# Two-layer hybrid encoder: the first product pair starts from the raw input, and the row factor goes into its eviction

## The chip, the core and the metric

One core of one Trainium2 chip runs the whole program. Its engines are named as in the profile: PE (TensorE, with PEld for its weight loads and PEq for its sequencer), DVE (VectorE), ACT (ScalarE), POOL (GpSimd) and SP (SyncE, which here only issues DMAs). The metric is the device time of one execution in microseconds (us), smaller is better. Before the change the median of three runs is 1521.92 us (1521.45 to 1524.45).

## The reference, cut to what matters

Two layers of one mixer. Each layer normalises the 512 x 2048 input by rows, multiplies it with one wide input projection, and runs three mixers on the parts. The change touches the beginning of layer 0 alone: the norm and the first part of the projection.

```python
def rmsnorm(x, g):
    x32 = x.astype(jnp.float32)
    y = x32 * lax.rsqrt(jnp.mean(x32 * x32, axis=-1, keepdims=True) + EPS)
    return (y * g.astype(jnp.float32)).astype(x.dtype)

h = rmsnorm(x, pre_norm_g[l])
z = h @ w_in[l]
q_lat, kv_lat, k_pe, gb, gc, xin, q_mem, gate = split_cols(z)
c_out = short_gated_conv(gb, gc, xin, conv_w[l])
```

The row factor (one number for each token, `r`) stands in front of a row of `h`. So a product of `h` with any block of `w_in` is the product of the unscaled rows with that block, each row of the result multiplied by its factor.

## The kernel before

**Numbers in two parts.** Every fp32 operand is split into a rounded part (`hi`, fp32r) and the rest (`lo`): ACT casts (L177 for weights, L257 for inputs), DVE subtracts (L178, L258). A product is three matmuls (`mm3`, L252 to L254): input hi x weight hi, input hi x weight lo, input lo x weight hi. The input tile is what PE loads (PEld), the 512 weight columns stream.

**Products.** The tokens are four tiles of 128; `x0` to `x3` in the code, t = 0 to 3. The projection is computed in groups of two column blocks with a seven-product scheme: the 2 x 2 blocks A11, A12, A21, A22 of the normalised transposed input (A11 = token tiles 0 and 1, first 1024 features; A12 = the same tokens, last 1024 features; A22 = token tiles 2 and 3, last 1024 features) and the sums S1 to S4 of them. Product P1 reads A11, P2 A12, P5 S1, P6 S2, P3 S4, P7 S3, P4 A22. Each product of a group is four steps (`c` = 0 to 3), each with one unit of weights of 256 rows by 512 columns (`wr` raw, `wh` and `wl` its parts) and 12 matmuls: 6 for the first token tile of the pair (`tt` = 0) and 6 for the second. For the first two groups, "first pair", the program runs P1 and P2 of group 0, then P1 and P2 of group 1, then P5 of group 0 and the rest. With `by_two` the first two steps of a product go together, so that 12 matmuls for tile 0 come before those for tile 1. Product P1 of such a group is copied out of PSUM by ACT (L464); the others are added by DVE.

**The beginning of layer 0.** PE runs 60 transposes of the identity (`warm`, L1208) while the input is on its way. For each token tile: SP loads all of `x` (L604), ACT sums the squares (L563), POOL makes `r` (L262, L264), DVE multiplies the rows by it (`hs`, L613, in halves of 1024), PE transposes quarters of four 128 x 128 blocks (`hps`, L582), and the eviction multiplies by the norm's gain (`hT`, by DVE L584 for token tiles 0 and 1, by ACT L588 for the second tile's first half and for tiles 2 and 3). Then A11 and A12 are split (L257, L258). The gains come from rows that ACT's queue loads (L281 to L283) and that one transpose turns (L291, L293).

**Order.** Each engine takes its own instructions strictly in the order of the program. PE, SP and POOL follow the order in which the steps are written (`add`, `put`); so do DVE and ACT until `first.close`, which stands behind the first step of P1. After that a scheduler orders DVE and ACT. Weight units are loaded 8 raw buffers deep, split two units ahead into 3 hi and 3 lo buffers; the sums S1 to S4 of token tiles 2 and 3 are put into a queue (`defer`) and given out between steps.

Of the kernel before, what the change touches and what calls it, by code (L numbers as in the profile page):

```python
# [5 lines left out]
F32 = mybir.dt.float32  # L6
# [6 lines left out]
P = 128  # L13
# [194 lines left out]
def encoder(tc, x, mem, positions, pre_norm_g, w_in, q_norm_g, w_uq, kv_norm_g, w_ukv, conv_w,  # L208
# [62 lines left out]
    def setup():  # L271
        ident = scrap("ident", P)
        make_identity(nc, ident)
        identr = const.tile([P, P], F32R, name="identr")
        nc.vector.tensor_copy(identr, ident)
# [3 lines left out]
        rows = scrap("rows", P)[:KT * 2 * depth + 12 * depth]  # L279
        n = KT * depth  # L280
        nc.scalar.dma_start(rows[:n], pre_norm_g.rearrange("l (k p) -> (l k) p", p=P))  # L281
        nc.scalar.dma_start(rows[n:2 * n], mem_norm_g.rearrange("l (k p) -> (l k) p", p=P))
        nc.scalar.dma_start(rows[2 * n:], conv_w.rearrange("l k (c p) -> (l k c) p", p=P))  # L283
        G["rows"] = rows

    def turn_constants():
        rows = G["rows"]
        n = KT * depth
        m = 2 * n + 12 * depth
        ps = bank("cps")  # L290
        nc.tensor.transpose(ps[:, :m], rows, G["ident"][:m, :m])  # L291
        cols = const.tile([P, m], F32, name="cols")
        nc.vector.tensor_copy(cols, ps[:, :m])  # L293
        for l in range(depth):
            G[f"g1_{l}"] = cols[:, l * KT:(l + 1) * KT]
            G[f"gm_{l}"] = cols[:, n + l * KT:n + (l + 1) * KT]
            G[f"cw{l}"] = cols[:, 2 * n + 12 * l:2 * n + 12 * (l + 1)].rearrange("p (k c) -> p k c", k=3)
# [72 lines left out]
    class Left:  # L370
# [8 lines left out]
        def split(self, name, p, src):  # L379
            t = self.ops[name, p] = slab(f"{name}{p}", F32R)  # L380
            c = src.shape[-1]
            split_to(t[:, :1024].rearrange("p (k c) -> p k c", c=c), t[:, 1024:].rearrange("p (k c) -> p k c", c=c), src)
# [33 lines left out]
    def group(left, key, w, block, slot, passes, final, hold=None, by_two=False):  # L416
# [185 lines left out]
    def first_load(t):  # L602
        xt = G[f"x{t}"] = slab("x")
        nc.sync.dma_start(xt, x[0, t * P:(t + 1) * P, :])  # L604
# [5 lines left out]
    def first_rows(t, halves=(0, 1)):  # L610
        for h in halves:
            c = slice(h * 1024, (h + 1) * 1024)
            nc.vector.tensor_scalar_mul(G[f"hs{t}"][:, c], G[f"x{t}"][:, c], G[f"r{t}"])  # L613


    def projection(l):
# [33 lines left out]
        def own_lat():  # L650
# [5 lines left out]
        L = G["left"]  # L656
        gs = [
            group(L, (l, 0), 512, block((O_GC, O_XI), 512), slot_of("gc", "xi"), HEAD, fin_u, by_two=l == 0),
# [445 lines left out]
    def out_proj(l):  # L1104
# [62 lines left out]
        g1 = group(G["left"], ("o", l, 1), 512, block(1), slot(1), LATE, fin(1), hold if last else None)  # L1167
# [72 lines left out]
    G["src"], G["dst"] = x[0], None  # L1240
    for l in range(depth):
# [7 lines left out]
        if l == 0:  # L1249
            add(use)  # L1250
            def turn_half(t, h, on=None):
                return lambda: transpose_rows(0, t, G[f"hs{t}"], (2 * h, 2 * h + 1), on)
# [29 lines left out]
        if l == 0:  # L1282
            put(a[:1])
            add(first.close)
            add(turn_half(1, 1))
            add(lambda: left_half(0, (1,)))
            add(lambda: left_half(1, (1,)))
            add(lambda: first_rows(2))
# [112 lines left out]
```

## Time and profile before

| | us |
|---|---|
| median of three runs | 1521.92 |
| the profiled execution's own time | 1524.04 |
| its span in the trace | 1522.3 |
| PE busy | 1491.2 |
| DVE busy | 1092.2 |
| ACT busy | 862.6 |

The span runs from the first to the last recorded instruction; 1.74 us of the profiled execution lie outside it. Times in the views are from the start of the span. A row of the timeline gives start, duration, engine, source line, operation, output and inputs, and in brackets how long the engine stood idle before and which instruction it waited for. Rows that overlap by a little are normal: an engine starts the next instruction before the last has drained, so that the distance between two starts, not the duration, is what a queue of them costs.

### The profile page before, as it was taken

The numbers are of one execution on the slowest core, as the hardware profiler recorded it, in microseconds if no ns is written. First come the engines' busy times: TensorE is split into PE (matmuls) and PEld (weight loads), VectorE is DVE, ScalarE is ACT, GpSimd is POOL, SyncE is SP. The second block draws the span as 40 slices with busy tenths as digits, with TensorE's granted clock in tenths as the row PEclk, the third lists the DMA queues.
The fourth block names the chain that finished last, engine by engine and source line by source line (L and its number), as shares of the span: only waits on it lengthen the run. The fifth ranks groups of instructions, "written<-read, shape, count | busy, mean of one in ns | idle before, by whom it ended". The sixth has DMA issues, their size and how long they took to land.

```text
span 1522.3 us, 20192 instructions
## 1 busy us (share of the span) xinstructions
PE 1491.2 (98%) x7613; PEld 1278.4 (84%) x7613; DVE 1092.2 (72%) x1446; ACT 862.6 (57%) x1335; POOL 258.6 (17%) x265
## 2 busy tenths in 40 slices
PE   9999999999999999999999999999999999998997
PEld 7788888988898888878788888888988888887885
DVE  6965675565968668979788766675566586698787
ACT  7733534454767768645688434434454686774543
POOL 1233131332000000010310333131332000000011
PEclk9999999999999999999999999999999999999999
DMA  8999898989581112165977999897999411022845
GB/s 332 217 221 223 197 173 172 204 192 261 155 273 59 42 42 71 35 164 156 322 277 247 236 229 226 183 177 167 195 211 221 130 59 40 29 84 62 240 100 180
DMA packets 138229, 258.80 MB, mean 170 GB/s; under 512 B 16828, under 2 KB 39700, under 8 KB 134804
## 3 DMA queue, kind: packets, MB, share of 16 engines
q0 software_dynamic: 52544, 116.41, 39.3%
q1 hardware_dynamic: 85456, 141.07, 28.7%
q8 instruction: 59, 0.97, 0.2%
q14 instruction: 38, 0.31, 0.1%
q10 hardware_dynamic: 132, 0.05, 0.0%
HBM read 242.81 MB, written 14.68 MB: 169 GB/s over the span
## 4 chain that ended last, share of the span: by engine, by line
PE 85%; DVE 7%; ACT 4%; issue 2%; DMA 2%; POOL 1%; DVEq 0%; POOLq 0%; ACTq 0%
PE P L253 20%; PE P L254 20%; PE P L252 20%; PE ptp L1002 2%; DVE wl L178 2%; PE tps L758 2%; DMA wr<-in_w_o_dram 1%; PE o L253 1%; PE sc L252 1%; PE sc L253 1%; PE sc L254 1%; PE o L254 1%; PE o L252 1%; PE sc L982 1%; PE sc L983 1%
## 5 line engine op out<-in xcount | busy, mean ns | idle before, releaser
L178 DVE TENSOR_TENSOR wl<-wr,wh 128x1024 fp32r<-128x1024 f32 (+1 forms) x400 | 475.8, 1195 | 286.5 <-ACT wh L177 284.6
L177 ACT CAST wh<-wr 128x1024 fp32r<-128x1024 f32 (+1 forms) x400 | 411.0, 1032 | 476.6 <-PE P L254 391.3
L253 PE MATMUL P<-wl,S 128*128 128x512 f32 (+1 forms) x896 | 345.2, 385 | 7.1 <-DVE wl L178 7.1
L252 PE MATMUL P<-wh,S 128*128 128x512 f32 (+1 forms) x896 | 347.0, 387 | 1.2 <-ACT wh L177 1.2
L254 PE MATMUL P<-wh,S 128*128 128x512 f32 (+1 forms) x896 | 344.0, 384 | 0.0
L137 POOL DMA_DIRECT2D wr<-in_w_in_dram x160 | 193.4, 1209 | 484.0 <-DVE wl L178 405.9
L252 PE MATMUL P<-wh,A 128*128 128x512 f32 (+1 forms) x656 | 253.1, 386 | 0.6 <-ACT wh L177 0.6
L253 PE MATMUL P<-wl,A 128*128 128x512 f32 (+1 forms) x656 | 251.9, 384 | 1.5 <-DVE wl L178 1.5
L254 PE MATMUL P<-wh,A 128*128 128x512 f32 (+1 forms) x656 | 251.7, 384 | 0.5 <-DVE A L258 0.5
L253 PEld LDWEIGHTS P<-wl,S 128*128 128x128 f32 x896 | 168.7, 188 | 39.0 <-DVE wl L178 9.7
L252 PEld LDWEIGHTS P<-wh,S 128*128 128x128 f32 x896 | 168.5, 188 | 31.7 <-ACT wh L177 2.2
L254 PEld LDWEIGHTS P<-wh,S 128*128 128x128 f32 x896 | 168.6, 188 | 30.5
L253 PEld LDWEIGHTS P<-wl,A 128*128 128x128 f32 x656 | 123.2, 188 | 23.7 <-DVE wl L178 2.1
L254 PEld LDWEIGHTS P<-wh,A 128*128 128x128 f32 x656 | 123.2, 188 | 23.3 <-DVE A L258 1.2
L252 PEld LDWEIGHTS P<-wh,A 128*128 128x128 f32 x656 | 123.1, 188 | 23.0 <-ACT wh L177 1.4
L988 ACT ACTIVATE P<-sc,nm 128x512 f32<-128x512 f32 (+1 forms) x96 | 59.9, 624 | 33.3 <-DVE nm L985 32.8
L1118 POOL DMA_DIRECT2D g<-in_post_norm_g_dram x8 | 5.5, 809 | 368.6 <-PE ptp L1002 368.6
L991 ACT ACTIVATE P<-P,rec 128x512 f32<-128x512 f32 (+1 forms) x96 | 62.1, 658 | 5.1 <-DVE rec L990 5.1
L985 DVE TENSOR_REDUCE nm<-sc 128x1 f32<-128x512 f32 (+1 forms) x96 | 57.3, 597 | 9.9 <-PE sc L983 6.3
L258 DVE TENSOR_TENSOR PT<-ptp,PT 128x512 fp32r<-128x512 f32 (+1 forms) x96 | 56.6, 595 | 4.9 <-ACT PT L257 4.5
L182 ACT ACTIVATE wh<-wr,cols 128x512 fp32r<-128x512 f32 x64 | 44.2, 721 | 20.0 <-PE mk L253 7.5
L183 DVE SCALAR_TENSOR_TENSOR wl<-wr,cols,wh 128x512 fp32r<-128x512 f32 x64 | 46.4, 750 | 12.3 <-ACT wh L182 10.9
(273 smaller groups left out, 2268.1 us busy)
## 6 DMA issues: line engine op xcount, KB each, us to landing
wr<-in_w_in_dram POOLq DMA_DIRECT2D x128, 512.0 KB, 6.9
wr<-in_w_in_dram SPq DMA_DIRECT2D x112, 512.0 KB, 5.6
wr<-in_w_o_dram SPq DMA_DIRECT2D x56, 512.0 KB, 4.6
wr<-in_w_in_dram POOLq DMA_DIRECT2D x32, 416.0 KB, 5.7
wr<-in_w_in_dram SPq DMA_DIRECT2D x24, 416.0 KB, 4.3
wr<-in_w_mk_dram SPq DMA_DIRECT2D x16, 512.0 KB, 5.1
wr<-in_w_mv_dram SPq DMA_DIRECT2D x16, 512.0 KB, 5.2
wr<-in_w_o_dram POOLq DMA_DIRECT2D x16, 512.0 KB, 7.0
```

Source lines behind the costliest of these rows:

```text
L137: engine.dma_start(dst, src, **kw)
L177: nc.scalar.copy(hi[:, :n], src)
L178: nc.vector.tensor_tensor(lo[:, :n], src, hi[:, :n].bitcast(F32), op=ALU.subtract)
L182: nc.scalar.activation(hi[:, h], src[:, h], AF.Copy, scale=g)
L183: nc.vector.scalar_tensor_tensor(lo[:, h], src[:, h], g, hi[:, h].bitcast(F32), op0=ALU.mult, op1=ALU.subtract)
L252: nc.tensor.matmul(ps, ah, bh, start=first, stop=False, **kw)
L253: nc.tensor.matmul(ps, ah, bl, start=False, stop=False, **kw)
L254: nc.tensor.matmul(ps, al, bh, start=False, stop=last, **kw)
L258: nc.vector.tensor_tensor(lo, src, hi.bitcast(F32), op=ALU.subtract)
L985: nc.vector.tensor_reduce(nmax, ps, axis=AX.X, op=ALU.max, negate=True)
L988: nc.scalar.activation(pt, ps, AF.Exp, bias=nmax, accum_out=tot)
L991: nc.scalar.activation(pt, pt, AF.Copy, scale=rec)
```

## The change

The names of the lines shift by up to 62 between the two programs; tile names stay.

- **Loads.** `x0` and `x1` are loaded in halves of 1024 features, and the weight units come between them: x0 first half, unit 0, x1 first half, unit 1, x0 second half, unit 2, x1 second half, unit 3, and so on. The gains of the memory norm and the convolution's weights move from ACT's queue to SP's, behind `x3`, and are turned later (`other_constants`, after P2 of group 0).
- **P1 of group 0** takes A11 from the raw, unscaled `x`, transposed and multiplied by the gain alone, and split by quarters. ACT's eviction of this product multiplies by `r` in place of a copy.
- **Factors.** The sums of squares of `x0` and `x1`, and the scaling of their second halves for A12, come after that.
- **A11 anew.** `spread_factors` builds, from diagonal matrices and a matrix of ones, a 128 x 256 tile of factors in PSUM by four matmuls (`rps`); `scale_half` multiplies the raw A11 (`hT`) by it on DVE, and A11 is split a second time for all products that follow.
- **PE.** 20 and 8 `warm` transposes in place of 60; the transposes of A12 come after the third step and after the last step of P1; `by_two` now also holds for P2 of group 0.

```diff
+        if len(halves) == 2:
+            nc.sync.dma_start(G[f"x{t}"], x[0, t * P:(t + 1) * P, :])
+        for h in halves if len(halves) == 1 else ():
+            c = slice(h * 1024, (h + 1) * 1024)
+            nc.sync.dma_start(G[f"x{t}"][:, c], x[0, t * P:(t + 1) * P, c])
...
-                if apart:
+                if apart and factor:
+                    nc.scalar.activation(s[1, 0], ps, AF.Copy, scale=factor(tt))
+                elif apart:
                     nc.scalar.copy(s[1, 0], ps)
...
-            if by_two and k == 0:
+            if by_two and k < 2:
...
+    def spread_factors():
+        ps = G["rows01"] = bank("rps")
+        for t in range(2):
+            work = scrap("diag", dt=F32R)
+            ones, dh, dl = (work[:, k * P:(k + 1) * P] for k in range(3))
+            d = scrap("factors", P)
+            nc.vector.tensor_scalar(ones, G["ident"], 0.0, 1.0, op0=ALU.mult, op1=ALU.add)
+            nc.vector.tensor_scalar_mul(d, G["ident"], G[f"r{t}"])
+            nc.vector.tensor_copy(dh, d)
+            nc.vector.tensor_tensor(dl, d, dh.bitcast(F32), op=ALU.subtract)
+            for k, part in enumerate((dh, dl)):
+                nc.tensor.matmul(ps[:, t * P:(t + 1) * P], ones, part, start=k == 0, stop=k == 1)
+
+    def scale_half(t):
+        h = G[f"hT{t}"][:, :8, :]
+        r = G["rows01"][:, t * P:(t + 1) * P].rearrange("p (o c) -> p o c", o=1).broadcast_to([P, 8, P])
+        nc.vector.tensor_tensor(h, h, r, op=ALU.mult)
...
+    add(lambda: first_load(0, (0,)))
+    add(pr.begin_loads(1))
+    add(lambda: first_load(1, (0,)))
+    add(pr.begin_loads(2))
     for t in range(2):
-        add(lambda t=t: first_load(t))
-        add(lambda t=t: first_factor(t))
-        if t == 0:
-            add(lambda: first_rows(0))
-    add(pr.begin_loads(3))
+        add(lambda t=t: first_load(t, (1,)))
+        add(pr.begin_loads(3 + t))
+    add(pr.begin_loads(6))
     add(lambda: first_load(2))
-    add(pr.begin_loads(5))
+    add(pr.begin_loads(8))
     add(lambda: first_load(3))
-    add(lambda: warm(60))
-    add(turn_constants)
+    add(constants_load)
+    add(lambda: warm(20))
+    add(pre_gains)
...
-            add(turn_half(0, 0))
-            add(lambda: first_rows(1, (0,)))
-            add(pr.begin_prep(1))
-            add(lambda: left_half(0, (0,)))
-            add(pr.begin_prep(2))
-            add(turn_half(1, 0, nc.scalar))
-            add(lambda: first_rows(1, (1,)))
-            add(lambda: left_half(1, (0,)))
-            add(pr.begin_prep(3))
-            add(lambda: first_factor(2))
-            add(turn_half(0, 1))
+            add(turn_raw(0, 0))
+            add(turn_raw(0, 1))
+            add(split_raw(0, 0))
+            add(pr.begin_prep(1))
+            add(split_raw(0, 1))
+            add(lambda: warm(8))
+            add(turn_raw(1, 0))
+            add(pr.begin_prep(2))
+            add(turn_raw(1, 1, nc.scalar))
+            add(split_raw(1, 0))
+            add(split_raw(1, 1))
+            add(pr.begin_prep(3))
+            add(lambda: first_factor(0))
...
             put(a[:1])
             add(first.close)
-            add(turn_half(1, 1))
-            add(lambda: left_half(0, (1,)))
-            add(lambda: left_half(1, (1,)))
-            add(lambda: first_rows(2))
-            add(lambda: first_factor(3))
-            add(lambda: first_rows(3))
-            put(a[1:], b[:1])
+            add(lambda: first_rows(0, (1,)))
+            add(lambda: first_factor(1))
+            add(lambda: first_rows(1, (1,)))
+            put(a[1:2])
+            add(turn_half(0))
+            add(lambda: left_half(0, (1,)))
+            put(a[2:])
+            add(turn_half(1))
+            add(lambda: left_half(1, (1,)))
+            add(spread_factors)
...
+            put(b[:1])
+            for t in range(2):
+                add(lambda t=t: scale_half(t))
+                add(lambda t=t: left_half(t, (0,)))
             add(turn[2])
             add(lambda: right_half(0))
-            put(b[1:3])
+            put(b[1:2])
             add(turn[3])
             add(lambda: right_half(1))
-            put(b[3:])
+            put(b[2:])
+            add(other_constants)
```

Three places show how DVE's queue moves. Names carry numbers that differ between the programs: `hT` is a transposed token tile, `A` a part of A11 or A12 (or A22), `S` a part of S1 to S4, `P` a product's PSUM bank.

DVE at its beginning; `hs` are scaled rows, `A` the low part of A11. Before:

```order
L613 TENSOR_SCALAR hs_102<-x_100,r_107 128x1024 x2
L293 COPY cols<-cps_195 128x88
L584 TENSOR_TENSOR hT_199<-hps_200,cols 128x512
L584 TENSOR_TENSOR hT_199<-hps_206,cols 128x512
L613 TENSOR_SCALAR hs_113<-x_111,r_118 128x1024
L178 TENSOR_TENSOR wl_214<-wr_120,wh_213 128x1024
L258 TENSOR_TENSOR A_20_217<-hT_199,A_20_217 128x1024
```

Now:

```order
L293 COPY colsrows<-cps_148 128x32
L598 TENSOR_TENSOR hT_152<-hps_153,colsrows 128x512
L598 TENSOR_TENSOR hT_152<-hps_159,colsrows 128x512
L258 TENSOR_TENSOR A_13_165<-hT_152,A_13_165 128x512
L641 TENSOR_SCALAR diag_334<-identr 128x128
L178 TENSOR_TENSOR wl_169<-wr_100,wh_168 128x1024
L258 TENSOR_TENSOR A_13_165<-hT_152,A_13_165 128x512
```

The two row scalings that waited for `r` are gone from the front; the first scaling now stands behind the third weight unit's low part.

DVE between the A12 splits and token tile 2's first work (`A_57` in the changed program, `A_50` before, is the part of A22 that is made from token tile 2). Before:

```order
L258 TENSOR_TENSOR A_38_324<-hT_224,A_38_324 128x1024
L613 TENSOR_SCALAR hs_329<-x_132,r_334 128x1024 x2
L178 TENSOR_TENSOR wl_363<-wr_272,wh_362 128x1024
L178 TENSOR_TENSOR wl_383<-wr_274,wh_382 128x1024
L178 TENSOR_TENSOR wl_444<-wr_276,wh_443 128x1024
L178 TENSOR_TENSOR wl_465<-wr_278,wh_464 128x1024
L258 TENSOR_TENSOR A_50_437<-hT_400,A_50_437 128x1024
```

Now:

```order
L258 TENSOR_TENSOR A_36_330<-hT_183,A_36_330 128x1024
L652 TENSOR_TENSOR hT_152<-hT_152,rps_333 128x1024
L632 TENSOR_SCALAR hs_350<-x_116,r_355 128x1024 x2
L652 TENSOR_TENSOR hT_183<-hT_183,rps_333 128x1024
L632 TENSOR_SCALAR hs_359<-x_122,r_364 128x1024 x2
L258 TENSOR_TENSOR A_13_165<-hT_152,A_13_165 128x1024
L258 TENSOR_TENSOR A_18_203<-hT_183,A_18_203 128x1024
L178 TENSOR_TENSOR wl_452<-wr_120,wh_451 128x1024
L178 TENSOR_TENSOR wl_456<-wr_221,wh_455 128x1024
L258 TENSOR_TENSOR A_57_445<-hT_408,A_57_445 128x1024
```

Two multiplications by the factors in PSUM and two more subtractions for A11 stand in front of the weights of P1 of group 1.

DVE in front of product P5 of group 0, whose second token tile reads `S_67` before and `S_77` now (S1 made from token tile 3). Before:

```order
L178 TENSOR_TENSOR wl_655<-wr_518,wh_654 128x1024
L397 TENSOR_TENSOR hT_481<-hT_481 128x1024
L397 TENSOR_TENSOR hT_481<-hT_224,hT_481 128x1024
L178 TENSOR_TENSOR wl_672<-wr_540,wh_671 128x1024
L258 TENSOR_TENSOR S_67_688<-hT_481,S_67_688 128x1024
```

Now:

```order
L178 TENSOR_TENSOR wl_650<-wr_511,wh_649 128x1024
L408 TENSOR_TENSOR hT_474<-hT_474 128x1024
L178 TENSOR_TENSOR wl_669<-wr_537,wh_668 128x1024
L408 TENSOR_TENSOR hT_474<-hT_183,hT_474 128x1024
L178 TENSOR_TENSOR wl_689<-wr_558,wh_688 128x1024
L469 TENSOR_TENSOR gb_535<-gb_535,P_71_629 128x512
L469 TENSOR_TENSOR gb_535<-gb_535,P_72_630 128x512
L178 TENSOR_TENSOR wl_708<-wr_580,wh_707 128x1024
L258 TENSOR_TENSOR S_77_720<-hT_474,S_77_720 128x1024
```

Two more weight units and two additions of P2's result now stand ahead of that S1 subtraction. Some 80 rows into DVE's queue, and at the matching places of the other engines, the two programs come to the same order and keep it to the end.

More of the change, by code (lines that the diff above doesn't have):

```diff
@@ L377, in __init__, with split @@
             self.ops = {}
-        def split(self, name, p, src):
-            t = self.ops[name, p] = slab(f"{name}{p}", F32R)
+        def split(self, name, p, src, ks=slice(None)):
+            if (name, p) not in self.ops:
+                self.ops[name, p] = slab(f"{name}{p}", F32R)
             c = src.shape[-1]
-            split_to(t[:, :1024].rearrange("p (k c) -> p k c", c=c), t[:, 1024:].rearrange("p (k c) -> p k c", c=c), src)
+            hi, lo = (self.ops[name, p][:, h * 1024:(h + 1) * 1024].rearrange("p (k c) -> p k c", c=c) for h in range(2))
+            split_to(hi[:, ks], lo[:, ks], src)
         def there(self, name, kt, tt):
@@ L414, in encoder, with group @@
     LATE = [["P2"], ["P1"], ["P5", "P6", "P3"], ["P7"], ["P4"]]
-    def group(left, key, w, block, slot, passes, final, hold=None, by_two=False):
+    def group(left, key, w, block, slot, passes, final, by_two=False, factor=None, hold=None):
         bk = {}
@@ L600, in right_half, with first_load @@
         combine(left, tt, a[:, :8, :], a[:, 8:, :], b[:, :8, :], b[:, 8:, :])
-    def first_load(t):
-        xt = G[f"x{t}"] = slab("x")
-        nc.sync.dma_start(xt, x[0, t * P:(t + 1) * P, :])
+    def first_load(t, halves=(0, 1)):
+        if f"x{t}" not in G:
+            G[f"x{t}"] = slab("x")
+        if len(halves) == 2:
[3 more added lines that the diff above has]
+            nc.sync.dma_start(G[f"x{t}"][:, c], x[0, t * P:(t + 1) * P, c])
     def first_factor(t):
@@ L656, in projection @@
         L = G["left"]
+        rf = (lambda tt: G[f"r{tt}"]) if l == 0 else None
         gs = [
-            group(L, (l, 0), 512, block((O_GC, O_XI), 512), slot_of("gc", "xi"), HEAD, fin_u, by_two=l == 0),
+            group(L, (l, 0), 512, block((O_GC, O_XI), 512), slot_of("gc", "xi"), HEAD, fin_u, l == 0, rf),
             group(L, (l, 1), 512, block((O_GB, O_G + 1024), 512), slot_of("gb", "gg"), HEAD, fin_g),
@@ L1166, in out_proj @@
         g0 = group(G["left"], ("o", l, 0), 512, block(0), slot(0), MERGED, fin(0))
-        g1 = group(G["left"], ("o", l, 1), 512, block(1), slot(1), LATE, fin(1), hold if last else None)
+        g1 = group(G["left"], ("o", l, 1), 512, block(1), slot(1), LATE, fin(1), hold=hold if last else None)
         return g0, g1, gains, fetch
```

42 lines of the change are left out of this document (26 added, 16 removed).

## The prediction

> **What bounds the kernel now.** I read the page's busy times first, then busy time in stretches of 10 us, then the timelines of PE, DVE and ACT up to 80 us, because from DVE's eightieth row on the two programs order their work alike. The page:
>
> ```profile
> span 1522.3 us, 20192 instructions
> PE 1491.2 (98%) x7613; PEld 1278.4 (84%) x7613; DVE 1092.2 (72%) x1446; ACT 862.6 (57%) x1335; POOL 258.6 (17%) x265
> ```
>
> Over the whole span PE is the bound: 31 us of its time are idle. The stage that is changed reads differently. Columns: the stretch, the sum, then busy PE, PEld, DVE, ACT, POOL (with counts), the granted PE clock, the DMA share, GB/s.
>
> ```profile
> 10.00:20.00 10.00, 7.92 (x50) 6.29 (x49) 8.73 (x12) 8.87 (x16) 0.74 (x2) 1.00 1.03 402
> ...
> 40.00:50.00 10.00, 9.05 (x39) 6.94 (x38) 9.65 (x10) 8.30 (x21) 2.62 (x2) 1.00 0.82 180
> 50.00:60.00 10.00, 10.00 (x46) 8.26 (x45) 9.65 (x10) 7.63 (x9) 2.43 (x2) 1.00 1.02 271
> 60.00:70.00 10.00, 10.00 (x46) 8.29 (x45) 9.93 (x10) 5.83 (x6) 3.62 (x3) 1.00 1.07 244
> 70.00:80.00 10.00, 10.00 (x46) 8.29 (x45) 9.55 (x10) 6.19 (x7) 3.68 (x4) 1.00 1.12 196
> 80.00:90.00 10.00, 10.00 (x46) 8.29 (x45) 4.90 (x4) 3.38 (x4) 4.80 (x4) 1.00 1.11 195
> ```
>
> From 40 to 80 us DVE is as full as PE; its first slack is 5.1 us at 80 to 90. So the beginning has two limits, PE's start and the sum of DVE's rows. The rows that fix them, first PE's:
>
> ```profile
> 1.61 4.70 PE L1208 MATMUL warm<-identr 128*128 128x128 f32 x21 [1.61 <-DVE identr L275]
> 1.61 8.96 PE L1208 MATMUL warm<-identr 128*128 128x128 f32 x60 [1.61 <-DVE identr L275]
> 13.13 1.96 PE L582 MATMUL hps<-identr,hs 128*128 128x128 f32 x16 [1.61 <-DVE hs L613]
> 14.85 0.47 PE L252 MATMUL P<-wh,A 128*128 128x512 f32 x1
> 27.66 0.39 PE L252 MATMUL P<-wh,A 128*128 128x512 f32 x1
> 49.12 0.50 PE L253 MATMUL P<-wl,A 128*128 128x512 f32 x1 [0.76 <-DVE wl L178]
> 65.14 0.39 PE L254 MATMUL P<-wh,A 128*128 128x512 f32 x1
> 65.36 0.39 PE L252 MATMUL P<-wh,S 128*128 128x512 f32 x1
> 76.24 0.39 PE L252 MATMUL P<-wh,S 128*128 128x512 f32 x1
> ```
>
> P1 starts at 14.85, P2 at 27.66, P5 of group 0 at 65.36 and P6 at 76.24; between matmuls lie 0.2267 us. Now DVE, from its first scaling to the subtraction for which P5's second token tile waits:
>
> ```profile
> 8.68 1.42 DVE L613 TENSOR_SCALAR hs<-x,r 128x1024 f32<-128x1024 f32 x2 [7.12 <-POOL r L264]
> 11.12 1.29 DVE L584 TENSOR_TENSOR hT<-hps,cols 128x512 f32<-128x512 f32 x2 [0.19 <-PE hps L582]
> 12.33 0.75 DVE L613 TENSOR_SCALAR hs<-x,r 128x1024 f32<-128x1024 f32 x1
> 12.99 1.22 DVE L178 TENSOR_TENSOR wl<-wr,wh 128x1024 fp32r<-128x1024 f32 x1
> 14.12 1.22 DVE L258 TENSOR_TENSOR A<-hT,A 128x1024 fp32r<-128x1024 f32 x1
> 37.03 1.23 DVE L178 TENSOR_TENSOR wl<-wr,wh 128x1024 fp32r<-128x1024 f32 x1 [2.95 <-ACT wh L177]
> 63.27 1.22 DVE L258 TENSOR_TENSOR S<-hT,S 128x1024 fp32r<-128x1024 f32 x1
> 64.40 1.22 DVE L178 TENSOR_TENSOR wl<-wr,wh 128x1024 fp32r<-128x1024 f32 x1
> 65.54 1.28 DVE L457 TENSOR_TENSOR gb<-gb,P 128x512 f32<-128x512 f32 x2
> ```
>
> The distance of starts is what a queue costs: 1.13 us for a subtraction of 1024 columns (12.99 to 14.12), 0.66 for a row scaling (12.33 to 12.99), 0.605 for an eviction of 512 (two in 11.12 to 12.33), 0.6 for a product's addition. That S1 subtraction ends at 64.5. P5's eighth matmul after its start is the first that reads it, at 65.36 + 8 x 0.2267 = 67.2. Before, DVE is 2.7 us ahead there.
>
> **The change part by part: PE's start.** Both loads and squares stand on ACT's timeline:
>
> ```profile
> 5.72 1.91 ACT L563 ACTIVATE hs<-x 128x2048 f32<-128x2048 f32 x1 [2.13 <-DMA x<-in_x_dram]
> 8.41 1.92 ACT L563 ACTIVATE hs<-x 128x2048 f32<-128x2048 f32 x1 [0.68 <-DMA x<-in_x_dram]
> 12.45 1.05 ACT L257 CAST A<-hT 128x1024 fp32r<-128x1024 f32 x1 [1.10 <-DVE hT L584]
> 13.40 1.06 ACT L177 CAST wh<-wr 128x1024 fp32r<-128x1024 f32 x1
> 31.83 4.24 ACT L588 ACTIVATE hT<-hps,cols 128x128 f32<-128x128 f32 x16
> 35.83 1.17 ACT L177 CAST wh<-wr 128x1024 fp32r<-128x1024 f32 x1
> ```
>
> `x0` is there at 5.72 and `x1` 2.69 us later, so half of `x0` should be there 1.35 us earlier, at 4.4. The 20 `warm` transposes last until about 6.0 (21 take 4.70 us); four transposes (0.5), an eviction (0.69 with 0.2 of wait) and the cast of a quarter (0.5, half of the 0.95 between 12.45 and 13.40) bring it to 8.0, unit 0's cast to 9.0: there the first matmul starts, in place of 14.85. That is 5.85 us for PE. Without them 1.4 us of PE work is added (8 `warm` at 0.11 by the rows above, 39 taking 4.26 us, and four small `rps` matmuls): if PE never waited for more than before, the kernel would gain about 4.9 us.
>
> It will wait, and I walked each in-order queue with those distances. The low part of unit 0 is ready at 10.3, of unit 1 at 12.6; the third step runs 16.5 to 19.2. The squares of `x0` stand on ACT behind three weight casts, so `r` of `x0` comes only at 16.4: the square starts at 13.4, and from a square's start to the scaling lie 2.96 us (5.72 to 8.68). The fourth step waits for its low part until 22.85. The `rps` matmuls of the second token tile wait for DVE's last diagonal row, which stands behind the evictions and the split of A12, until 26.5; P2, behind them on PE, starts at 26.75 and not at 27.66. So the 5.85 us have shrunk to 0.9. In P1 of group 1 the second token tile needs the PSUM bank that P2's additions free, at 44.2; its last low part is ready at 51.85. P5 starts at 65.3, level with before.
>
> **DVE's sum.** Before, 55.7 us pass from 8.68 to 64.40. In them stand 17 weight subtractions, 11 of inputs and 6 combinations (L397), 34 x 1.135 = 38.6; 8 scalings, 5.4; 6 evictions, 3.6; 2 additions, 1.2; `cols`, 0.25. Some of these groups, up to 66 us, with the count, busy us and mean ns, and the idle time before them with its cause (the eighteenth weight subtraction is the one at 64.40):
>
> ```profile
> L178 DVE TENSOR_TENSOR wl<-wr,wh 128x1024 fp32r<-128x1024 f32 x18 | 21.7, 1220 | 3.5 <-ACT wh L177 3.5
> L613 DVE TENSOR_SCALAR hs<-x,r 128x1024 f32<-128x1024 f32 x8 | 5.7, 750 | 8.0 <-POOL r L264 8.0
> L275 DVE CAST identr<-ident 128x128 fp32r<-128x128 f32 x1 | 0.2, 228 | 1.3 <-POOL ident masks.py:199 1.3
> L293 DVE COPY cols<-cps 128x88 f32<-128x88 f32 x1 | 0.2, 250 | 0.6 <-PE cps L291 0.6
> ```
>
> Together 49.0; 6.7 us are waits and gaps. Now, to the same subtraction:
>
> - added: two multiplications by the factors. No row of before multiplies 1024 columns by a PSUM operand. Nearest are the eviction (0.605 for 512, so 1.21) from above and 1.135 from below; I take 1.2 each: +2.4.
> - two more A11 subtractions, done first by quarters: 4 quarters at 0.57 (half of 1.135) instead of none, while the two whole ones stay: +2.3.
> - eight rows of 128 x 128 for the diagonals: such a cast lasts 0.23 (`identr`), and starts lie up to 0.1 closer than durations (0.66 against 0.75 for a scaling), so 0.13 to 0.23; I take 0.175: +1.4, 1.0 to 1.8.
> - one eviction more (+0.6), a second `cols` (+0.2), two row scalings less (-1.3).
> - two weight subtractions and two additions now stand ahead of this row that stood behind it: 2 x 1.135 + 2 x 0.6 = +3.5.
>
> That is 58.0, 9.0 more, of which 5.5 is new work and 3.5 moved. DVE begins, with `cols`, at 6.3, when `warm` and its transpose are over, and not at 8.68: -2.4. Its waits I put at 4.8 instead of 6.7: 0.6 before the first weight, 1.6 for `r` of `x0`, 0.4 for `r` of `x1` and 0.4 for that of `x2`, 1.5 for a weight whose cast stands on ACT behind the 16 evictions that take 4.0 us at 31.83, 0.3 for the rest. So the subtraction ends at 6.3 + 58.0 + 4.8 + 0.1 = 69.2 against the 65.3 + 1.8 = 67.1 at which P5 needs it: PE stands for 2.1 us, in a place where it did not stand before.
>
> What the change does to SP's queue costs nothing:
>
> ```profile
> 5.72 0.34 SPq L604 DMA_DIRECT2D x<-in_x_dram x1
> ```
>
> four issues more take 1.4 us while the transfers, 2.69 us for 1 MB, are the slower part and hide them (uncovered, 1.4 us), and the gains that leave ACT's queue are needed only after P2. What waits behind P5's matmul on PE is everything to the end of layer 0, so the delay stays. The two weights and two additions are already done then, so DVE itself is only 4.7 - 3.5 = 1.2 late afterwards, less than PE, and the 5.1 us of slack at 80 to 90 take that up. The price of the change is 2.1 - 0.06 = +2.0 us.
>
> **By the Trainium skill.** The PE clock opened during `warm`: 0.224 us each for the first 21, 0.109 for the other 39. The Trainium skill, "TensorE: Matmul & The Clock Gate", Part 4, says that the clock gate does not engage for transposes, which do not count as busy; by that 20 transposes would open nothing and the first matmuls would run at half pace. The trace disagrees: it opened with transposes alone.
>
> **Rivals.**
>
> R1, DVE hardly waits. If the squares and casts of ACT come early enough, the early start is kept: with no wait at all the subtraction ends at 64.4, PE meets P5 unhindered, and what remains is DVE's bound, 4.8 us below the forecast: -2.8; with half of my waits, -0.4. 1519.1 to 1521.5. For it: ACT loses the two squares from its front. Against: `r` feeds two scalings and a diagonal now, and ACT is 8.3 of 10 busy at 40 to 50.
>
> R2, slower: the PE clock closes in the sparse stretch between 9 and 27, where PE has to stand six times, up to 2.5 us at `rps`. Half pace costs 0.11 us a transpose in `warm`'s first part, and if 20 matmuls of 0.2267 run so, 4.5 us; half of that lies in waits anyway. P2 starts 2.2 later, and so do the evictions on which DVE works: 2.0 + 2.2 = +4.2, 1526.1. Against: the 1.61 us gap at 11.5 to 13.1 left the clock at 1.00. The Trainium skill, same page, Part 1, has the gate fall back after an idle window of some 3.4 us; no gap in my walk is that long, so by it R2 would not happen.
>
> R3, slower: DVE's waits stay at 6.7, since ACT's 16 evictions and the later `r` hold it as the 2.95 us at 37.03 did; DVE is 1.9 us later still, with the small rows at 0.23 2.3: +3.9 to +4.3, 1526.0. It decides from 1 us of wait above mine. For it: ACT's rows in front of DVE's weights are more, not fewer.
>
> R4, the halves do not land early: `x0`'s first half arrives at 5.7 as the whole does. `warm` covers to 6.0, DVE's first eviction comes 1.0 to 1.3 later: +3.2, 1525.1.
>
> **Numbers.** Forecast 0.43, R1 0.20, R2 0.10, R3 0.22, R4 0.05. The profiled execution took 1524.04, 2.1 above the median of 1521.92; the sum is a difference (span 1522.3 to 1524.3), so I add it to the median: 1523.9. Its own range is 1522.4 to 1525.4 (small rows, scalings and the waits' 1 us either way). Range for 8 in 10: 1519.8 to 1526.6, which leaves out R1's far end and R3's and R2's. A measurement of this kernel tells 0.2%, 3.0 us, from no change. Faster than that: 0.07, from R1's end with shorter rows. Slower: 0.08 of the forecast, R2, 0.20 of R3, 0.03 of R4: 0.41. Same: 0.52.
>
> **What would show it.** First matmul of P1 near 9.0; P2 near 26.8 behind a PE gap at `rps` that DVE releases; in P1 of group 1 a wait for DVE's additions; DVE at 9.5 or more of 10 from 40 to 80; P5 near 65.3, and in it a wait of about 2 us for DVE's L258 ending near 69.2; after 90 us the same stalls, 2 us later. I am wrong if P5's second tile does not wait, or if P6 starts at or before 76.2, where it stood.

## The result, and the profile after

Over 16 executions of each kernel the median went from 1524.09 to 1526.49 us, 2.4 apart, and the mean from 1523.60 to 1526.66, 3.1 apart; the ratio is 1.0020, as that of the means, with a 95% interval of 1.0012 to 1.0028. On the first median of 1521.92 that is 1525.0 us, 3.0 slower (1.8 to 4.3). The forecast was 1523.9. The page of the changed kernel:

```profile
span 1523.3 us, 20162 instructions
PE 1487.5 (98%) x7586; PEld 1273.4 (84%) x7586; DVE 1097.3 (72%) x1460; ACT 864.3 (57%) x1335; POOL 258.1 (17%) x265
```

DVE works 5.1 us more, PE 3.7 less. Busy time by stretches, in the columns of before:

```profile
40.00:50.00 10.00, 8.74 (x38) 6.63 (x37) 10.00 (x12) 8.25 (x22) 2.62 (x2) 1.00 0.74 176
50.00:60.00 10.00, 9.78 (x44) 7.77 (x43) 10.00 (x10) 8.73 (x11) 2.43 (x2) 1.00 1.05 259
60.00:70.00 10.00, 8.23 (x37) 6.50 (x36) 9.96 (x11) 4.12 (x4) 3.62 (x3) 1.00 1.10 276
...
80.00:90.00 10.00, 10.00 (x46) 8.29 (x45) 6.62 (x6) 4.30 (x5) 4.01 (x5) 1.00 1.09 184
```

DVE is now full from 40 to 70, and it is PE that has holes: 1.77 us of 60 to 70, where it had none. PE's timeline shows them one by one:

```profile
9.04 0.48 PE L252 MATMUL P<-wh,A 128*128 128x512 f32 x1
...
26.72 0.33 PE L646 MATMUL rps<-diag 128*128 128x128 f32 x1 [2.20 <-DVE diag L644]
26.88 0.45 PE L252 MATMUL P<-wh,A 128*128 128x512 f32 x1
...
44.56 0.50 PE L252 MATMUL P<-wh,A 128*128 128x512 f32 x1 [1.26 <-DVE gc L469]
52.10 0.50 PE L253 MATMUL P<-wl,A 128*128 128x512 f32 x1 [0.22 <-DVE wl L178]
...
65.61 0.39 PE L252 MATMUL P<-wh,S 128*128 128x512 f32 x1
...
69.36 0.50 PE L254 MATMUL P<-wh,S 128*128 128x512 f32 x1 [1.77 <-DVE S L258]
...
78.60 0.39 PE L252 MATMUL P<-wh,S 128*128 128x512 f32 x1
```

P1 starts 5.8 us earlier (9.04 for 14.85), P2 0.8 earlier, P5 0.25 later, and P6 at 78.60 for 76.24: 2.36 us late. From there both programs run alike; matched instruction by instruction the distance is 2.36 at 100 us and 2.62 at 1390. On DVE and ACT:

```profile
39.28 1.23 DVE L178 TENSOR_TENSOR wl<-wr,wh 128x1024 fp32r<-128x1024 f32 x1 [1.61 <-ACT wh L177]
...
68.09 1.22 DVE L258 TENSOR_TENSOR S<-hT,S 128x1024 fp32r<-128x1024 f32 x1
```
```profile
34.09 4.23 ACT L602 ACTIVATE hT<-hps,colsrows 128x128 f32<-128x128 f32 x16
38.10 1.15 ACT L177 CAST wh<-wr 128x1024 fp32r<-128x1024 f32 x1
```

The S1 subtraction ends at 69.31. DVE's last pause before it is the 1.61 us at 39.28, behind the 16 evictions.

The two spans differ by 1.0 us only. The profiled execution of before lost time near its end, and its granted clock over the span is 0.996, against 0.998 for the changed kernel's. Two stretches of 3.41 us there, of before:

```profile
1402.19:1405.60 3.41, 1.63 (x6) 1.13 (x7) 3.41 (x4) 1.74 (x2) 0.92 (x1) 1.00 0.00 0
1405.60:1409.01 3.41, 3.41 (x9) 2.64 (x8) 2.72 (x3) 0.57 (x1) 0.29 (x1) 0.50 0.69 139
```

PE was idle for 1.78 us and the granted clock was 0.50 right behind. In every other profile of this study PE makes good 1.2 to 2.5 us against that one execution between 1390 and 1405 us. Where the clock stays open there it makes good some 1.6 more behind it, of which 0.9 to 1.1 is lost again by 1420. All those profiles are of the changed kernel or its variants, so whether the kernel before always loses this time is not shown by traces. So the start of P6 and the ratio measure a change here, and a pair of spans doesn't.

### The profile page after: what moved, and what is told of

Same layout as the page of the kernel before. It is cut to its first block, busy times and chain, and to the rows that moved or that the text cites. A ratio compares the mean times of both kernels' runs of the same rounds, so it can differ in the third digit from the quotient of the medians.

```text
span 1523.3 us, 20162 instructions
## 1 busy us (share of the span) xinstructions
PE 1487.5 (98%) x7586; PEld 1273.4 (84%) x7586; DVE 1097.3 (72%) x1460; ACT 864.3 (57%) x1335; POOL 258.1 (17%) x265
## 4 chain that ended last, share of the span: by engine, by line
PE 78%; DVE 9%; ACT 4%; DMA 4%; issue 3%; POOL 1%; DVEq 0%; POOLq 0%; ACTq 0%
PE P L253 18%; PE P L254 18%; PE P L252 18%; DVE wl L178 3%; PE ptp L1042 2%; DMA wr<-in_w_o_dram 2%; PE tps L798 1%; DMA wr<-in_w_in_dram 1%; PE o L253 1%; PE sc L252 1%; PE sc L253 1%; PE sc L254 1%; PE o L254 1%; PE o L252 1%; PE sc L1022 1%
## 5 line engine op out<-in xcount | busy, mean ns | idle before, releaser
L182 ACT ACTIVATE wh<-wr,colsmore 128x512 fp32r<-128x512 f32 x64 | 44.2, 721 | 20.0 <-PE mk L253 7.7
L183 DVE SCALAR_TENSOR_TENSOR wl<-wr,colsmore,wh 128x512 fp32r<-128x512 f32 x64 | 46.2, 745 | 12.4 <-ACT wh L182 12.2
```

Of the source, the lines that this page charges most:

```text
L182: nc.scalar.activation(hi[:, h], src[:, h], AF.Copy, scale=g)
L183: nc.vector.scalar_tensor_tensor(lo[:, h], src[:, h], g, hi[:, h].bitcast(F32), op0=ALU.mult, op1=ALU.subtract)
```

## The experiments

"P6" is the start of P6 of group 0 in the profile (76.24 before), "stall" the wait in P5's second token tile, "closed" the start of a period at half clock before 100 us, as explained below. Each ratio is to executions of the kernel before that ran beside that run; ratios of different rows come from different chips and differ less surely.

| run | P6 | stall | closed at | ratio to before, interval |
|---|---|---|---|---|
| changed kernel | 78.60 | 1.77 | none | 1.0020 (1.0012 to 1.0028) |
| e11, the same again | 81.44 | 1.77 | 27.3 and 71.6 | 1.0017 (1.0008 to 1.0025) |
| e1, no rescaling | 79.34 | 1.77 | 27.5 | 1.0006 (0.9997 to 1.0015) |
| e2, split twice | 82.17 | 2.51 | 27.2 and 71.6 | 1.0027 (1.0017 to 1.0037) |
| e3, rps later | 78.11 | 2.02 | none | 1.0006 (0.9996 to 1.0015) |
| e4, resplit late | 78.85 | 1.77 | 69.5 | 1.0010 (0.9999 to 1.0021) |
| e8, gap filled | 80.45 | 1.77 | 71.2 | 1.0027 (1.0017 to 1.0037) |
| e10, both gaps filled | 78.47 | none | none | 1.0008 (0.9999 to 1.0016) |
| e5, e3 + e4 | 76.74 | 1.77 | none | 1.0005 (0.9995 to 1.0016) |
| e6, e5 + constants late | 76.84 | 1.55 | none | 1.0004 (0.9996 to 1.0013) |
| e7, e6 + square first | 76.80 | 1.55 | none | 1.0004 (0.9993 to 1.0014) |
| e9, x2 early | 81.46 | 1.55 | 50.6 | 1.0021 (1.0013 to 1.0030) |
| e12, P5 by two steps | 78.38 | 0.41 | 27.1 | 1.0006 (0.9997 to 1.0015) |
| e13, e6 + e12 | 75.71 | 0.18 | none | 1.0005 (0.9996 to 1.0014) |
| e14, resplit behind P6 | 76.11 | 0.20 | none | 1.0038 (1.0024 to 1.0052) |
| e15, P2 by single steps | 79.06 | none | 27.3 | 1.0011 (1.0002 to 1.0019) |
| e16, e15 + late parts | 77.33 | none | none | 1.0009 (1.0000 to 1.0019) |

**e1: no rescaling of A11**, which stays without its factor for all that follows P1 of group 0. Each of the two token tiles loses:

```diff
-                add(lambda t=t: scale_half(t))
-                add(lambda t=t: left_half(t, (0,)))
```

> The two multiplications of A11 by the row factors and the second split of A11 are left out, so A11 stays without its factor for everything after P1 of group 0. That takes 2 x 1.13 + 2 x 1.14 = 4.5 us off DVE and 1.9 us off ACT before the S1 subtraction that P5 waits for. If the sum of DVE's rows sets the price (theory): the subtraction ends near 65 instead of 69.3, PE does not stand in P5, P6 starts between 75.0 and 76.5 instead of 78.6, and the ratio to the kernel before lies between 0.999 and 1.001. If the price comes from PE's own gaps at the beginning (rival): P6 stays at 78.6, ratio 1.002.

The ratio of 1.0006 is the theory's, but its profile did not come: P6 started at 79.34, and the subtraction ended at 70.07, later than in the changed kernel.

```profile
41.02 1.23 DVE L178 TENSOR_TENSOR wl<-wr,wh 128x1024 fp32r<-128x1024 f32 x1 [3.85 <-ACT wh L177]
...
68.85 1.22 DVE L258 TENSOR_TENSOR S<-hT,S 128x1024 fp32r<-128x1024 f32 x1
```

With 4.5 us of rows gone, DVE waits 3.85 us instead of 1.61 for the weight behind the 16 evictions, and runs without a pause from there, as before. Those evictions were late because token tile 2 was transposed at 34.63 for 32.39: P2's first matmuls stood 0.43 us apart in that execution, at half clock, which blurs the comparison. Had the transposes come at 32.39 as in the changed kernel, the weight would stand near 38.8 (an estimate, 41.02 less the 2.24 that they were late), 0.5 us earlier for 4.5 us of rows. So rows ahead of 39 us are largely covered by ACT and PE; the sum over all of DVE's rows is not by itself the price.

**e2: A11 split once more.**

```diff
+            for t in range(2):
+                add(lambda t=t: left_half(t, (0,)))
```

> A11 is split a third time with the same result: 2 x 1.14 = 2.3 us more on DVE and 1.9 us more on ACT ahead of the S1 subtraction, nothing on PE. Theory (DVE's sum sets the end): each added microsecond arrives, the stall in P5 grows from 1.8 to about 4.1, P6 starts near 80.9, ratio to the kernel before 1.0035. Rival (PE's own gaps): DVE's rows hide, P6 stays at 78.6, ratio 1.002.

P6 came at 82.17 in an execution that closed its clock twice. Against e11, which closed at the same two places, the wait of P5's second tile ended at 71.40 for 70.60: of 2.3 us added 0.8 arrived there. Theory had all of it arrive, and a ratio of 1.0035 for the 1.0027 measured: half a confirmation. The scheduler had also put one combination (L408, 1.13 us) behind that subtraction that stood ahead of it in the changed kernel, so some 1.1 us were left to arrive, and the rest is again a sign of cover.

**e3, e4, e5: the factor matmuls later, the second split later, both.** e3 moves one line, e4 gives the second group the factor too and puts the split behind P5 (`first_a` holds A11's scaled halves); e5 does both.

```diff
-            add(spread_factors)
             add(lambda: first_factor(2))
...
             put(b[:1])
+            add(spread_factors)
...
-            group(L, (l, 1), 512, block((O_GB, O_G + 1024), 512), slot_of("gb", "gg"), HEAD, fin_g),
+            group(L, (l, 1), 512, block((O_GB, O_G + 1024), 512), slot_of("gb", "gg"), HEAD, fin_g, False, rf),
...
+            first_a = {}
             for t in range(2):
+                add(lambda t=t: first_a.update({t: G[f"hT{t}"][:, :8, :]}))
                 add(lambda t=t: scale_half(t))
-                add(lambda t=t: left_half(t, (0,)))
...
-        put(*gs[0][2:], *gs[1][2:])
+        put(gs[0][2])
+        if l == 0:
+            for t in range(2):
+                add(lambda t=t: pr.defer(1.2, lambda: G["left"].split("A11", t, first_a[t])))
+        put(*gs[0][3:], *gs[1][2:])
+        if l == 0:
+            add(pr.settle)
```

> The four small matmuls that spread the factors move on PE from ahead of P2 to behind its first two steps; DVE's rows are the same. The gap of 2.2 us in front of them goes, and P2 starts near 24.5 instead of 27. Theory (DVE's sum): the S1 subtraction still ends near 69.3, so P6 starts at 78.6 within 0.4, and the ratio stays 1.002. Rival (PE's own gaps set the price): P6 starts near 76.4, ratio 1.0005.

> P1 of group 1 takes the raw A11 too, with the factor in its eviction, and the second split of A11 moves behind P5 of group 0, where DVE had 5 us of slack before. 2.3 us leave DVE and 1.9 leave ACT ahead of the S1 subtraction. Theory: it ends near 67.0, the stall in P5 falls from 1.8 to below 0.4, P6 starts between 76.0 and 76.7, and the ratio to the kernel before is 1.000 within 0.001. Rival (PE's own gaps): P6 stays at 78.6, ratio 1.002. A second rival: the moved rows are late where they now stand, and PE loses the same 2 us between 80 and 140 us.

> Second split of A11 behind P5 of group 0, P1 of group 1 from the raw A11, and the factor matmuls behind P2's first two steps, so that the gap of 2.2 us and 2.3 us of DVE's rows are both gone from the stretch ahead of P5. If DVE's rows and PE's gap act in one chain (P2's start, token tile 2's transposes, ACT's 16 evictions, a weight's low part, then DVE without a pause): P5's second tile is reached at 66.0 to 67.5 instead of 69.4, P6 starts between 75.2 and 76.8, ratio 0.9995 to 1.0005. If only DVE's sum counts: 76.3, ratio 1.000. If neither: 78.6, 1.002.

Alone, e3 brings P6 0.5 us forward (the theory allowed 0.4, the rival 2.2), while its ratio fell as the rival said; e4 leaves P6 where it was, at a clock that closed behind P5's stall. The theory had that stall fall below 0.4; it stayed at 1.77 and only ended 1.3 us earlier, at 68.05. Together they bring P6 to 76.74, inside the range for one chain of PE, ACT and DVE. The stall is still there, but P5 starts at 63.76:

```profile
67.50 0.51 PE L254 MATMUL P<-wh,S 128*128 128x512 f32 x1 [1.77 <-DVE S L258]
```

The table shows the same 1.77 us in six profiles. In all six, 17.2 to 17.3 us lie between the last low part that PE waits for in P1 of group 1 (52.10 in the changed kernel, 50.24 in e5) and the end of the stall (69.36 and 67.50). DVE's rows between the two set the stall, so what is saved ahead of them moves both ends alike; e12 and e15 below test that.

**e11 and e10: the clock.** e11 is the changed kernel, e10 adds 18 and 16 transposes of the identity in PE's two longest gaps:

```diff
+            if t == 1:
+                warm(18)
             for k, part in enumerate((dh, dl)):
...
+                    if q == "P5" and key == (0, 0) and c == 0 and tt == 1:
+                        warm(16)
                     products(q, c, tt, ops[0])
```

> The changed kernel once more, as the measure for the next one on the same chip. Expected: P6 between 78.5 and 79.3 where the clock stays at 1.00 in P5, 1.7 us later where it closes behind the stall; ratio to the kernel before 1.0015 to 1.0028.

> The changed kernel with 18 transposes of the identity on PE in the gap ahead of the second pair of rps matmuls and 16 more (16 x 0.11 = 1.8 us) ahead of the second token tile of P5's first step, where PE stood for 1.77 us; they wait for nothing and nothing waits for them but PE itself. Clock theory: no period of the record's clock closes before 300 us, so each execution loses the 2.4 us of the profile and not 1.7 more in some of them: ratio 1.0013 to 1.0018, 0.0004 to 0.0010 below the changed kernel run beside it, P6 at 78.6 to 79.2. Rival (closings in these two places are rare or hidden): both ratios agree within 0.0003.

The same four stretches of the changed kernel's first profile, then of e11:

```profile
24.00:27.27 3.27, 1.07 (x9) 0.88 (x7) 3.27 (x6) 2.81 (x4) 0.00 (x0) 1.00 1.04 374
27.27:30.68 3.41, 3.41 (x17) 2.83 (x16) 3.08 (x4) 3.41 (x4) 0.74 (x2) 1.00 1.05 386
68.00:71.64 3.64, 2.28 (x10) 1.87 (x11) 3.57 (x4) 1.03 (x2) 1.20 (x1) 1.00 1.13 210
71.64:75.06 3.42, 3.42 (x17) 2.82 (x16) 3.02 (x4) 2.02 (x3) 1.22 (x1) 1.00 1.10 202
```
```profile
24.00:27.27 3.27, 1.07 (x11) 0.93 (x9) 3.27 (x7) 2.81 (x5) 0.00 (x0) 1.00 1.03 373
27.27:30.68 3.41, 3.41 (x9) 2.74 (x10) 3.29 (x3) 3.41 (x4) 0.57 (x2) 0.50 1.05 386
68.00:71.64 3.64, 1.87 (x9) 1.23 (x8) 3.58 (x4) 0.15 (x1) 1.74 (x2) 1.00 1.11 252
71.64:75.06 3.42, 3.42 (x10) 2.66 (x9) 3.39 (x4) 1.99 (x2) 0.44 (x1) 0.50 1.13 207
```

One program, two executions: in e11 the granted clock (third column from the right) is 0.50 for 3.41 us behind each of the two gaps, and 9 and 10 matmuls pass where 17 did. PE in e11:

```profile
27.21 0.45 PE L646 MATMUL rps<-diag 128*128 128x128 f32 x1 [2.20 <-DVE diag L644]
...
70.60 0.50 PE L254 MATMUL P<-wh,S 128*128 128x512 f32 x1 [1.77 <-DVE S L258]
...
72.03 0.63 PE L253 MATMUL P<-wl,S 128*128 128x512 f32 x1
72.46 0.63 PE L254 MATMUL P<-wh,S 128*128 128x512 f32 x1
...
81.44 0.39 PE L252 MATMUL P<-wh,S 128*128 128x512 f32 x1
```

Matmuls 0.43 us apart, and P6 at 81.44 where it was 78.60. Of these 2.84 us 0.5 were there ahead of P2 already (the `rps` matmul at 27.21 for 26.72; the record's clock opens at 6.79 us for 4.62, during `warm`), 0.75 came up to the end of the stall in P5 (70.60 for 69.36), behind the first closing, and 1.60 behind the second. With both gaps filled the clock stayed at 1.00 in the same stretches of e10:

```profile
27.27:30.68 3.41, 3.41 (x16) 2.81 (x15) 3.08 (x4) 3.41 (x4) 0.74 (x2) 1.00 1.05 388
...
71.64:75.06 3.42, 3.42 (x16) 2.81 (x15) 3.05 (x4) 1.91 (x2) 1.22 (x1) 1.00 1.09 199
```

P6 came at 78.47. The ratio is 0.0009 below that of e11 run beside it, as expected of the difference, though 1.0008 lies below its own range, which began at 1.0013. The two intervals overlap, so the size is less sure than the mechanism. The mechanism has a second witness, the granted clock over the whole span, which is on record for every execution: it is 0.997 or more in 11 of e10's 12 executions, and in 4 of e11's 12.

**e8: the first gap alone filled** (the first of e10's two edits).

> Like the changed kernel, with 18 more transposes of the identity on PE in the gap ahead of the second pair of rps matmuls (18 x 0.11 = 2.0 of its 2.2 us); DVE, ACT and P2's start stay. Clock theory: where PE is idle for more than about 1.8 us inside one 3.4 us period of the clock's record, the next period runs at half pace (1.7 us lost); this gap closes the clock in some executions of the changed kernel and in none of this one, so the ratio falls from 1.002 by 0.0003 to 0.0007 and the spread of the times narrows. Rival (the closings cost nothing, since DVE and ACT set P5 anyway): ratio unchanged at 1.002, and P6 at 78.6 in the profile whether the clock closed or not.

A miss: the ratio did not fall. P5's stall was left, and closed the clock in the profile (P6 at 80.45). The changed kernel did not run beside this one, and e8 was slower at the same granted clock too (1526.45 us in its two executions at 0.998, 1524.66 in six of the changed kernel), which stays open. Whether filling the first gap alone is worth anything is not shown.

**e6, e7, e9: more moved on top of e5.** `other_constants` behind P2 of group 1 (e6); also the square of `x0` ahead of the third weight cast (e7). e9 is e6 with the square of `x2` ahead of A12's work on ACT, and the second split held behind P5's result:

```diff
+                one = small()
+                nc.vector.tensor_scalar(one, C["xi"][:, 2 + t, :1], 0.0, 1.0, op0=ALU.mult, op1=ALU.add)
+                nc.scalar.activation(hi, first_a[t], AF.Copy, scale=one)
```

> Like the one before, and the gains of the memory norm and the convolution are turned only after P2 of group 1, so that P1 of group 1 need not wait for P2's additions to free a PSUM bank (1.26 us in the changed kernel). Expected: P1 of group 1 without that wait, P6 at 75.0 to 76.5, ratio 0.9990 to 1.0003. Rival: DVE has no pause from 34 on, the wait only moves to P5, and P6 and ratio equal those of the kernel without this step.

> Like the one before, and on ACT the sum of squares of x0 stands ahead of the third weight cast, so that its factor is ready about 1 us earlier and DVE's wait of 1.6 us for it goes. If DVE's early waits are passed on: P6 0.8 to 1.5 us earlier than in the kernel without this step, ratio 0.9985 to 0.9997. If ACT's 16 evictions set the pace after 30 us: P6 within 0.3 us of it.

> P1 of group 1 from the raw A11, the factor matmuls behind P2's first two steps, the second split of A11 held behind P5's result by a scale of 1.0 that is made from it, the convolution's gains turned after P2 of group 1, and the sum of squares of x2 ahead of the A12 work on ACT. Against the kernel with three steps moved this takes DVE's waits of 1.47 and 0.71 us for the factors of x2 and x3, and DVE ran without a pause from there to the S1 subtraction. If those waits set its end: the subtraction ends near 65.5 instead of 67.6, PE stands for less than 0.3 us in P5, P6 starts between 74.8 and 75.6 (76.24 before), ratio 0.9990 to 0.9998. If something else holds it: P6 stays at 76.8, ratio 1.0004.

e6 and e7 change nothing, as their second cases had it: the wait for a bank was gone in e5 already, and the earlier factor of `x0` is not passed on. e9 missed by 6 us: PE waited 1.22 us for a weight's cast on ACT at 49.23, the clock closed at 50.6, and P5 started only at 68.59; what held the rest was not followed up.

**e12 and e13: P5's need moved.**

```diff
-            if by_two and k < 2:
+            if by_two and k < 3:
```

> The changed kernel, with the first two steps of P5 of group 0 taken together as those of P1 and P2 are: 12 matmuls of token tile 0 stand ahead of tile 1 instead of 6, so the S1 subtraction is needed 6 x 0.2267 = 1.36 us later; DVE's rows ahead of it stay the same and it still ends near 69.3. If the lateness of that one row against P5 is the whole price: the stall in P5 falls from 1.77 to about 0.4, too short to close the clock, P6 starts near 77.3, ratio 1.0003 to 1.0010. If the price comes from elsewhere: P6 at 78.6 or later, ratio 1.0017 to 1.0020.

> The same for the kernel with three steps moved late, whose stall in P5 was 1.55 us and whose P6 started at 76.84. Expected: a stall of 0.2 us, P6 near 75.5 (76.24 before), ratio 0.9993 to 1.0000, faster than both kernels. If P5's second weight unit is late instead: a wait for a weight's low part inside P5 and P6 at 76.5 or later, ratio 1.0003.

In e12 the stall is 0.41, as worked out from 1.77 - 1.36; P6 came 1.1 later than expected, as P5 started that much later behind a clock that had closed ahead of P2, and the ratio lies in its range. In e13 P5 hardly waits and P6 starts at 75.71, 0.5 us ahead of the kernel before; the ratio of 1.0005 misses its range all the same. Behind P6:

```profile
77.95 0.50 PE L252 MATMUL P<-wh,S 128*128 128x512 f32 x1 [0.73 <-ACT S L257]
79.45 0.50 PE L254 MATMUL P<-wh,S 128*128 128x512 f32 x1 [0.77 <-DVE S L258]
```

The next sums are late in their turn, and at 100 us PE is 1.52 behind the kernel before.

**e14, e15, e16.** e14 is e13 with the split held behind P6's result in e9's way; e15 undoes only P2's steps (`by_two and k == 0`, `b[1:3]`, `b[3:]`); e16 is e6 with those and P5 by two.

> P5's first two steps together, the factor matmuls behind P2's first two steps, P1 of group 1 from the raw A11, the convolution's gains later, and the second split of A11 held behind P6's result by a scale of 1.0 made from it, so that its two subtractions (2.3 us of DVE) stand behind 85 us and no longer ahead of the sums for P6 and P3. If DVE's rows up to P6 were all that was still late: no stall in P5 over 0.3, the stalls of 0.73 and 0.77 in P6 and P3 go, PE at 100 us is 0.2 to 1.0 us ahead of the kernel before, ratio 0.9990 to 1.0000. If the rows come late again where they now stand: PE is 1 us or more behind at 140 us, ratio 1.0005 as without this step.

> The changed kernel with one part undone: P2 of group 0 goes step by step as before the change, token tile 2 is transposed behind its first step and tile 3 behind its third. The scheduler then puts the S1 subtraction for P5's second tile ahead of the two weights and two additions that stood ahead of it in the changed kernel (3.5 us). If that order is the price: the subtraction ends near 66 instead of 69.3, P5 starts near 65.5 and its second tile does not wait, P6 starts between 76.2 and 76.8, ratio 1.0000 to 1.0007 (the gap ahead of P2 and its closings stay). If the new work on DVE is the price whatever the order: P6 at 78.6, ratio 1.0017 to 1.0020.

> P2 step by step as before the change, P5's first two steps together, the factor matmuls behind P2's first step, P1 of group 1 from the raw A11 with the second split later, and the convolution's gains later. Expected if the order is the price and P2's early start is then kept: no stall in P5, P6 between 74.7 and 75.6 (76.24 before), PE at 100 us between 1.0 us ahead of the kernel before and 0.3 behind, ratio 0.9990 to 1.0002. If DVE's rows only come late further on (as two waits of 0.75 us in P6 and P3 showed): PE 1.5 us behind at 100, ratio 1.0005.

e14 is within 0.4 us of before up to 98 us (P6 at 76.11, no stall over 0.2), but the scheduler put P7's sum behind the held split. PE stood 2.94 us for it at 102.82, the clock closed for two periods, and at 140 us PE is 7.6 behind. e15 frees P5 of its stall, as expected of the order, but P6 at 79.06 and the ratio of 1.0011 miss the ranges of that case; P5 itself starts at 68.18, part of it the closing ahead of P2, part a new wait in P1 of group 1:

```profile
51.95 0.50 PE L253 MATMUL P<-wl,A 128*128 128x512 f32 x1 [1.47 <-DVE wl L178]
```

So P2 by two steps does set that order, and undoing it moves the same lateness to the weights. e16 follows its second case. No run beat the kernel before; the best, e5 to e7 and e13, cannot be told from it, their intervals like several others including 1.

## Why the prediction was right or wrong

The place, the order of the waits and the direction were right. First matmul 9.0, measured 9.04. The gap at `rps`, forecast up to 2.5 us: 2.20. P2 at 26.75: 26.88. Wait for P2's additions until 44.2: 44.56. The last low part, 51.85: PE resumes at 52.10. P5 65.3: 65.61. End of the S1 subtraction 69.2: 69.31. P6, from 76.24 + 2.0: 78.2, measured 78.60. The sum was 0.36 short there: P5's start was put at -0.06 and is +0.25.

What failed is the step from P6 to the time of an execution. "PE stands for 2.1 us" was priced as standing alone, with nothing for the clock. R2, the closing clock, was looked for between 9 and 27 only, given 0.10, and argued down because the gap of 1.61 us had left the clock at 1.00. That was no bound, and R2 came in some executions, in P5 as well as at `rps`. In the profiles of this study the clock's record runs in periods of 3.413 us whose beginning differs from one execution to the next. Before 1511 us, 19 periods held 1.77 us or more of idle PE and were followed by one at half clock; three with 1.77, 1.82 and 1.90 were not; of the periods at full clock with 1.75 or less none was. The 1.61 us of before had been cut by a boundary into at most 1.44 in one period. The changed kernel has two gaps on or above that line, 2.20 at `rps` and 1.77 in P5, and its two profiles close behind both or neither; variants closed behind one alone (e1 at 27.5, e8 at 71.2). By the matmuls 0.43 us apart a closing costs up to half a period, 1.7 us (an estimate); behind P5's stall 1.60 were measured. The Trainium skill, "TensorE: Matmul & The Clock Gate", Part 1, has this free-running period (4096 cycles, 3413 ns), and the trace agrees with its length; it asks for an idle period, a rule that the prediction leant on against R2, and here a little over half of one was enough (1.77 us of 3.413).

How often each gap closes over the executions was not measured, but their granted clocks size the step. Among executions at 0.998, the highest on record and so those with the fewest periods at half clock, the changed kernel takes 1524.66 us on average (6) and the kernel before 1522.64 (44): 2.0 apart, the forecast's own number. Over all of them the changed kernel averages 0.9963 (28) and the kernel before 0.9969 (145). Of 1524 us that is 0.9 us of clock (an estimate; the executions come from several chips), the part that the sum lacked. The chance of 0.52 for "within 0.2%" rested on the 2.0 us alone. A term of about 1 us for the clock would have put the forecast on the bound of 0.2%, and slower ahead of same.

A second step holds less than it seemed to: "the sum of DVE's rows". It gave the right end, 69.2 for 69.31, in part by luck: DVE's `cols` began 0.6 us earlier than assumed (5.67 for 6.3), the waits were 4.6 us where 4.8 were assumed, and the rows with the small gaps between them took 59.1 where the sum had 58.1. And e1 shows that rows ahead of 39 us can go with little gain, as ACT's evictions and PE's transposes hold the next weight; what counts is the time of that weight and the 28.8 us of rows without a pause behind it. e5, which frees both, takes the price from 2.36 to 0.5.

R1 did not come: DVE waited. R3's waits of 6.7 us did not either. R4 neither: the halves landed in time.

## What to carry to other kernels

An earlier start is worth only what the next full engine lets through: here 5.8 us at the first matmul were used up before 66 us, and each reordering brought the same lateness out at another wait. Where PE gets a new gap, price it twice: its length, and, once it exceeds about half a clock period (1.77 of 3.413 us in these traces), up to half a period more in some executions. Compare kernels by an instruction from which both run alike and by many executions; a single pair of spans differed here by 1.0 us where the change was worth 2.4 and more.

## What was not expected of the hardware

Two executions of one program differ by 2.84 us at the same instruction, and 2.35 of that came up behind two half-clock periods that one has and the other has not. Transposes open that clock and keep it open: in the kernel before it opened during `warm`, at 6.14 us, and in e10 18 and 16 of them in the gaps kept it at 1.00. A multiplication of 1024 columns with a PSUM operand took 1.21 us, no more than one from SBUF (1.22).
